# Down projections of four f blocks as seven products of halves in a hybrid decoder kernel

## The chip, the cores and the metric

The kernel runs on one core of a Trainium2 chip. The metric is the device time of one execution in microseconds (us); a profiled execution shows what each engine of the core did in it. The engines are TensorE (PE, with its weight loads as PEld), VectorE (DVE), ScalarE (ACT), GpSimd (POOL) and SyncE (SP), which here only issues DMAs.

## The reference, cut to what matters

Two decoder layers over 528 tokens (16 meta tokens and 512 others) with 1024 features. Each layer has an attention part, which the change leaves alone, and then a gated feed-forward part of 2816 hidden features, all in float32:

```python
h = h + mix @ w_out                                    # end of the attention part
hn = rmsnorm(h, ffn_norm)
ff = silu(hn @ w_gate) * (hn @ w_up)                   # 528 x 2816
h  = h + ff @ w_down                                   # 528 x 1024
```

After the second layer comes a last rmsnorm, and the meta tokens are dropped.

## The kernel before

Everything is kept transposed: features on the 128 partitions, tokens along the free axis. `h` is eight tiles of 128 x 528. The hidden features are 22 blocks of 128, called f; an output block of 128 features is called m. In the first layer a product covers 528 tokens, in two column halves of w = 264. In the second layer only the 512 real tokens count (w = 256).

A float32 product is made as three matmuls of rounded numbers. A weight tile or an activation is split into a high part (`hi`, a rounding copy on ACT) and a low part (`lo`, source minus high part, a subtraction on DVE or POOL), and hi x hi, hi x lo and lo x hi are added in PSUM. All "splits" below are such a pair: one ACT copy, then one DVE subtraction that waits for it.

The feed-forward part goes through `ROUNDS`: f blocks 0-2, 3-6, 7-10, 11-14, 15-18 and 19-21. The first three are computed plainly. Each later f is a `Unit`, which computes gate and up together: the 2 x 2 block product (two halves of the 1024 input features, two halves of the tokens, gate and up as the two outputs) is made by seven products instead of eight. The products are numbered 1, 2, 6, 5, 7, 4, 3 in the order in which they run; each is 12 matmuls. The banks are called x (products 1, 6, 7 and 4 add into it, and `keep` copies it out on ACT in between), z and y. `done` of a unit then adds the pieces, applies the scale `R` and silu, multiplies gate by up and splits the result into the activation tiles `ah` and `al` (f mod 8).

The down projection of a round is done while the next round's units run: a `down_job` loads the weights of two output blocks m for the round's f blocks, splits them, and `down` makes one m: for each f three passes over all tokens. In the first layer that is two 264-column matmuls per pass, in the second layer one of 512 columns. With four f blocks a pair of m takes 48 matmuls of 264 columns, or 24 of 512. Its result goes to an `S` tile (ACT) and is added to `h` by an accumulating DMA from GpSimd's queue. In the last round of units the addition is done by DVE, and the last round's own three f blocks are added after all units. The order before is: products 1, 2, 6, 5, 7 of the unit; first m; products 4 and 3 of the unit; second m.

The weights pass through jobs: `need(j)` loads and converts job j and the next two. A job's `hi` and `lo` live in two rings of two buffers each (`whi`, `wlo` and `fwhi`, `fwlo`, used in turn), so four jobs are alive at a time, and a fifth conversion waits until PE has finished the job four places before. The raw weights have a ring of three (`raw`), two (`fraw`) and two (`Sw`). For each unit two sums of weights are made by accumulating DMAs from GpSimd's queue (into `Sw` and `fraw`); DVE makes two more (`make2`, `make4`).

Tiles, slots and the order on each engine come from a scheduler that works on the program order and priorities; within an engine everything runs strictly in the order so fixed. PSUM has two double banks (`psd`) and four single banks (`psa`).

Of the kernel before, what the change touches and what calls it, by code (L numbers as in the profile page):

```python
# [10 lines left out]
F32 = mybir.dt.float32  # L11
# [28 lines left out]
def hybrid_kernel(ctx, tc, x_t, w_in, w_fl, w_out, w_gate, w_up, w_down, vecs, b_fg, rope, decay, mask, ident, out_t):  # L40
# [753 lines left out]
    def ffn(l, st, real, last):  # L794
# [6 lines left out]
        held = []  # L801
# [3 lines left out]

        def act_tile(f):
            return fft(f"ah{f % 8}"), fft(f"al{f % 8}")
# [80 lines left out]
        class Unit:  # L888
            def __init__(self, f):
                self.f = f  # L890
                self.t = {}
                self.w1 = add_job(load=self.load, make=self.make1, n=NK)

            def rest(self):
                self.w2 = add_job(load=self.load, make=self.make2, n=NK)
                self.w3 = add_job(load=self.load, make=self.make3, n=NK)

            def last(self):
                self.w4 = add_job(load=self.load, make=self.make4, n=HB)
# [15 lines left out]
            def make2(self, hi, lo):  # L915
                a, s = self.t["a"], self.t["s"]
                nc.vector.tensor_add(s[:, 0:HB], s[:, HB:NK], a[:, 0:HB])  # L917
# [8 lines left out]
            def make4(self, hi, lo):  # L926
                a, s = self.t["a"], self.t["s"]
                nc.vector.tensor_add(a[:, HB:NK], a[:, HB:NK], s[:, 0:HB])
                splits(hi, lo, a[:, HB:NK])
# [23 lines left out]
            def done(self):  # L953
# [12 lines left out]
                fh, fl = act_tile(self.f)  # L966
                split(fh[:, c], fl[:, c], u[:, c])
                acts[self.f] = (fh, fl)
# [12 lines left out]
            def tail(self):  # L981
                x, y = (self.bank(n) for n in "xy")
                return (product(self.w3, HB, t_form(3), x, False, True)
                        + product(self.w4, 0, x_block(1, 1), y, False, True, done=self.done))

# [51 lines left out]
        fills = []  # L1037
        for r, (f0, f1) in enumerate(ROUNDS):
            for f in range(f0, f1):
# [4 lines left out]
                u = Unit(f)  # L1044
# [16 lines left out]
            for p, g0, g1 in fills:  # L1061
                j = down_job(p, g0, g1)
# [353 lines left out]
```

## Time and profile before

| | before |
|---|---|
| median of 3 runs | 1272.64 us (1271.05 to 1273.75) |
| the profiled execution | 1271.96 us |
| its span | 1270.1 us |
| PE busy | 1255.0 us (99% of the span) |
| DVE busy | 914.1 us (72%) |
| ACT busy | 720.6 us (57%) |
| POOL busy | 386.2 us (30%) |
| first layer's feed-forward part | about 316 us, from 330 us to 646 us |
| second layer's | about 290 us, from 950 us to 1240 us |

The span is the time from the first to the last instruction in the profile; 1.9 us of the execution lie outside it. Busy time is the time in which an engine executes at least one instruction. Matmuls overlap in the array, so how long one takes in a row of them is read from the distance between their starts, and not from its own duration.

### The profile page before, as it was taken

The numbers are of one execution on the slowest core, as the hardware profiler recorded it, in microseconds if no ns is written. First come the engines' busy times: TensorE is split into PE (matmuls) and PEld (weight loads), VectorE is DVE, ScalarE is ACT, GpSimd is POOL, SyncE is SP. The second block draws the span as 40 slices with busy tenths as digits, with TensorE's granted clock in tenths as the row PEclk, the third lists the DMA queues.
The fourth block names the chain that finished last, engine by engine and source line by source line (L and its number), as shares of the span: only waits on it lengthen the run. The fifth ranks groups of instructions, "written<-read, shape, count | busy, mean of one in ns | idle before, by whom it ended". The sixth has DMA issues, their size and how long they took to land.

```text
span 1270.1 us, 24076 instructions
## 1 busy us (share of the span) xinstructions
PE 1255.0 (99%) x9271; PEld 1196.9 (94%) x9271; DVE 914.1 (72%) x1689; ACT 720.6 (57%) x1326; POOL 386.2 (30%) x662
## 2 busy tenths in 40 slices
PE   9999999999999999999999999999999999999997
PEld 8999999999999999999999989998789999999996
DVE  8877756779766666666786877477896666666766
ACT  7666545676555555554456665557765555555544
POOL 3355546421122222220025545554202222222100
PEclk9999999999999999999999999999999999999999
DMA  6322222225687777774323222222358887787721
GB/s 218 94 72 86 88 84 77 66 68 164 173 189 184 184 184 184 182 182 120 100 77 118 68 97 79 84 83 67 126 144 196 185 196 184 184 189 184 171 78 67
DMA packets 71315, 167.53 MB, mean 132 GB/s; under 512 B 8208, under 2 KB 15120, under 8 KB 71200
## 3 DMA queue, kind: packets, MB, share of 16 engines
q1 hardware_dynamic: 50576, 128.70, 31.7%
q0 software_dynamic: 20160, 36.97, 17.9%
q8 instruction: 73, 1.20, 0.4%
q14 instruction: 42, 0.34, 0.1%
q10 hardware_dynamic: 464, 0.32, 0.1%
HBM read 146.79 MB, written 2.13 MB: 117 GB/s over the span
## 4 chain that ended last, share of the span: by engine, by line
PE 92%; DVE 3%; DMA 2%; ACT 2%; issue 0%; DVEq 0%
PE psd L217 29%; PE psa L881 19%; PE psd L1016 14%; PE psd L881 13%; PE psa L217 5%; PE psa L1016 4%; PE psa L418 2%; PE psa L573 2%; PE psa L507 2%; PE psa L730 1%; PE psa L700 1%; DMA raw<-w_in 0%; DMA dec<-decay 0%; ACT whi L191 0%; PE psa L290 0%
## 5 line engine op out<-in xcount | busy, mean ns | idle before, releaser
L194 POOL TENSOR_TENSOR wlo<-raw,whi 128x128 fp32r<-128x128 f32 x504 | 259.1, 548 | 287.9 <-ACT whi L191 287.8
L217 PE MATMUL psd<-xh,whi 128*128 128x264 f32 (+1 forms) x792 | 195.8, 315 | 0.4 <-ACT whi L191 0.4
L217 PE MATMUL psd<-xh,wlo 128*128 128x264 f32 (+1 forms) x792 | 186.7, 303 | 0.0
L217 PE MATMUL psd<-xl,whi 128*128 128x264 f32 (+1 forms) x792 | 186.2, 302 | 0.4 <-DVE xl L320 0.4
L217 PEld LDWEIGHTS psd<-xh,whi 128*128 128x128 f32 x792 | 128.3, 189 | 5.4 <-ACT whi L191 1.1
L217 PEld LDWEIGHTS psd<-xh,wlo 128*128 128x128 f32 x792 | 127.0, 188 | 6.3 <-DVE wlo L194 0.4
L217 PEld LDWEIGHTS psd<-xl,whi 128*128 128x128 f32 x792 | 127.6, 189 | 4.7 <-DVE xl L320 0.8
L191 ACT CAST whi<-raw 128x512 fp32r<-128x512 f32 (+1 forms) x168 | 98.4, 613 | 49.6 <-PE psd L217 37.4
L908 POOL DMA_DIRECT2D Sw<-w_up x38 | 34.2, 899 | 230.5 <-DMA Sw<-w_up 146.4
L909 POOL DMA_DIRECT2D fraw<-w_gate x38 | 33.3, 875 | 210.5 <-DMA fraw<-w_up 65.9
L870 DVE TENSOR_TENSOR fwlo<-raw,fwhi 128x1024 fp32r<-128x1024 f32 (+2 forms) x62 | 64.0, 1033 | 38.1 <-ACT fwhi L869 38.0
L870 DVE TENSOR_TENSOR wlo<-raw,whi 128x1024 fp32r<-128x1024 f32 (+2 forms) x62 | 62.9, 1015 | 36.7 <-ACT whi L869 36.5
L869 ACT CAST whi<-raw 128x1024 fp32r<-128x1024 f32 (+2 forms) x62 | 54.9, 885 | 46.2 <-PE psd L881 37.0
L869 ACT CAST fwhi<-raw 128x1024 fp32r<-128x1024 f32 (+2 forms) x62 | 55.6, 897 | 42.8 <-PE psd L881 36.7
L917 DVE TENSOR_TENSOR Sw<-Sw,raw 128x512 f32<-128x512 f32 x38 | 26.3, 692 | 72.4 <-DMA raw<-w_gate 71.4
L1026 POOL DMA_DIRECT2D h<-S x64 | 59.9, 936 | 50.1 <-ACT S L1023 26.8
L881 PE MATMUL psa<-th,whi 128*128 128x264 f32 (+1 forms) x232 | 65.5, 283 | 0.0
L881 PE MATMUL psa<-th,wlo 128*128 128x264 f32 (+1 forms) x232 | 65.4, 282 | 0.0
L881 PE MATMUL psa<-tl,whi 128*128 128x264 f32 (+1 forms) x232 | 65.3, 282 | 0.0
L881 PE MATMUL psa<-th,fwhi 128*128 128x264 f32 (+1 forms) x224 | 63.5, 283 | 0.3 <-ACT e L947 0.3
L881 PE MATMUL psa<-tl,fwhi 128*128 128x264 f32 (+1 forms) x224 | 63.3, 283 | 0.0
L881 PE MATMUL psa<-th,fwlo 128*128 128x264 f32 (+1 forms) x224 | 63.2, 282 | 0.0
(344 smaller groups left out, 4027.3 us busy)
## 6 DMA issues: line engine op xcount, KB each, us to landing
raw<-w_in SPq DMA_DIRECT2D x54, 512.0 KB, 3.5
raw<-w_gate SPq DMA_DIRECT2D x44, 512.0 KB, 6.4
fraw<-w_up SPq DMA_DIRECT2D x38, 512.0 KB, 5.6
raw<-w_down SPq DMA_DIRECT2D x64, 256.0 KB, 2.9
Sw<-w_up SPq DMA_DIRECT2D x38, 256.0 KB, 2.6
fraw<-w_gate POOLq DMA_DIRECT2D x38, 256.0 KB, 4.3
Sw<-w_up POOLq DMA_DIRECT2D x38, 256.0 KB, 6.0
h<-S POOLq DMA_DIRECT2D x32, 264.0 KB, 5.5
```

Of the source, the lines that this page charges most:

```text
L191: pin(nc.scalar.copy(hi, job["raw"][:, c0:c1]), pinned)
L194: pin(sub(lo[:, i:i + step], job["raw"][:, c0 + i:c0 + i + step], hi[:, i:i + step].bitcast(F32)), pinned)
L217: nc.tensor.matmul(ps[1][b][:, 0:c1 - c0], w[:, wk, :], x[:, c0:c1], start=(k == 0 and i == 0), stop=(k == n - 1 and i == 2))
L418: nc.tensor.transpose(ps[:, 128 * j:128 * j + 128], src[:, o:o + 128], idt)
L869: nc.scalar.copy(hi, src)
L870: nc.vector.tensor_sub(lo, src, hi.bitcast(F32))
L881: nc.tensor.matmul(bank()[:, 0:b.shape[-1]], a[:, o + k, :], b, start=(fresh and k == 0 and i == 0), stop=(k == n - 1 and i == 2), skip_gr ...
L908: nc.gpsimd.dma_start(s[:, HB:NK], w_up[l, self.f][:, 0:HB], accum_op=ALU.add)
L909: nc.gpsimd.dma_start(self.t["b"][:, 0:HB], w_gate[l, self.f][:, 0:HB], accum_op=ALU.add)
L917: nc.vector.tensor_add(s[:, 0:HB], s[:, HB:NK], a[:, 0:HB])
L1016: nc.tensor.matmul(v[:, 0:c1 - c0], a[:, s * n + k, :], b[:, c0:c1], start=(k == 0 and i == 0), stop=(k == n - 1 and i == 2))
L1026: nc.gpsimd.dma_start(two(h[m]), c, accum_op=ALU.add)
```

## The change

Down projections of the four rounds with four f blocks (3-6, 7-10, 11-14, 15-18) are also made as a 2 x 2 block product by seven products. One `Down` covers two output blocks m (the two row halves), the even and the odd f blocks of the round (the inner halves; `w_down` is laid out in the order 0, 2, 1, 3 on the host for this) and the two halves of the tokens. Each product has two f blocks, so 6 matmuls; seven make 42. What this takes:

- Activations: for each pair of f blocks seven blocks of w columns are stored as hi and lo instead of four: the first unit's first half, both halves of the second unit, and four sums, which DVE makes (`done`: one subtraction after the first unit, three after the second). The splits cover 7 w per pair instead of 4 w.
- Weights: seven blocks of 128 x 256 instead of four. GpSimd makes three sums, as six additions of 128 x 128 (`Down.load`); DVE makes one, of 128 x 256 (`make_b`). The splits cover 1792 columns (two of 512, one of 768) instead of 1024. A `Down` is two jobs instead of one.
- Results: four ACT copies of w columns, one DVE addition of y to one of them (`keep`), and one DVE addition of z and y (`done`), before the accumulating DMAs to `h`, which stay two per pair. They are now also used in the last round of units, except for its last pair.
- Order: the products of the unit and of the `Down` alternate, as the tuples in the loop say; for the first pair of a round the last two products of the `Down` come after product 1 of the next unit. `need` looks three jobs ahead instead of two.
- A unit's `make4` addition is moved into `make2`; the raw gate weights have no later reader then.

```diff
         def need(j):
-            for i in range(j, min(j + 3, len(jobs))):
+            for i in range(j, min(j + (4 if jobs[j].get("far") else 3), len(jobs))):
...
                 nc.vector.scalar_tensor_tensor(lo, s, -1.0, hi.bitcast(F32), ALU.mult, ALU.subtract)
+                nc.vector.tensor_add(s[:, 0:HB], a[:, HB:NK], s[:, 0:HB])
...
             def make4(self, hi, lo):
-                nc.vector.tensor_add(a[:, HB:NK], a[:, HB:NK], s[:, 0:HB])
-                splits(hi, lo, a[:, HB:NK])
+                splits(hi, lo, self.t["s"][:, 0:HB])
...
+                q, second = divmod(self.f - PLAIN, 2)
+                if not second:
+                    us[q] = u2, two(tt("tq"))
+                    nc.vector.tensor_sub(us[q][1][:, 0], u2[:, 1], u2[:, 0])
+                    return
+                u0, ta = us.pop(q)
+                tb = two(tt("tq"))
+                parts = [(0, 1, u0[:, 0:1]), (1, 2, u2), (3, 2, ta), (5, 2, tb)]
+                for i, (s, n, src) in enumerate(parts):
+                    if i == 2:
+                        nc.vector.tensor_sub(tb[:, 0], u2[:, 1], ta[:, 0])
+                        nc.vector.tensor_sub(tb[:, 1], u2[:, 1], u0[:, 1])
+                        nc.vector.tensor_sub(ta[:, 1], u2[:, 0], tb[:, 0])
+                    ph, pl = slots(q, s, n, 0), slots(q, s, n, 1)
...
+        class Down:
...
+                for k in range(2):
+                    nc.gpsimd.tensor_add(sd[:, 2 + k], r[:, 4 + k], r[:, 6 + k])
+                for k in range(2):
+                    nc.gpsimd.tensor_sub(sd[:, k], sd[:, 2 + k], r[:, k])
+                for k in range(2):
+                    nc.gpsimd.tensor_sub(r[:, 4 + k], r[:, k], r[:, 4 + k])
+
+            def make_a(self, hi, lo):
+                splits(hi[:, 0:HB], lo[:, 0:HB], self.t["r"][:, 0:HB])
+                splits(hi[:, HB:NK], lo[:, HB:NK], self.t["s"])
+
+            def make_b(self, hi, lo):
+                r = self.t["r"]
+                nc.vector.tensor_sub(r[:, 2:4], r[:, 2:4], self.t["s"][:, 0:2])
+                splits(hi, lo, r[:, 2:NK])
...
+                        nc.scalar.copy(e, self.t["x"][:, 0:w])
+                        if i == 3:
+                            nc.vector.tensor_add(e, self.t["y"][:, 0:w], e)
...
+                    nc.vector.tensor_add(e, self.t["zy"][:, :, 0:w], e)
...
+                    if p == 0:
+                        order = ((u, 1), (u, 2), (u, 6), (u, 5), (u, 7), (d, 1), (d, 2), (u, 4), (d, 6), (d, 5), (u, 3), (d, 7))
+                    else:
+                        order = [(u, 1)] + hang + [(u, 2), (d, 1), (u, 6), (d, 2), (u, 5), (d, 6), (u, 7), (d, 5), (d, 7),
+                                                   (u, 4), (d, 4), (d, 3), (u, 3)]
+                    hang = [(d, 4), (d, 3)] if p == 0 else []
```

Three places show how the instructions now stand.

On DVE before, in the first layer, after a unit's up half is read from PSUM (L964, L965): w4's low part (L870 with 512 columns), the split of the activation (L143), then weights again.

```order
L964 TENSOR_TENSOR tq_5519<-psa_5365,tq_5519 128x264
L965 TENSOR_TENSOR tq_5519<-e_5378,tq_5519 128x264
L870 TENSOR_TENSOR fwlo_5620<-raw_5444,fwhi_5619 128x512
L143 TENSOR_TENSOR al7_5524<-tq_5519,ah7_5523 128x528
L870 TENSOR_TENSOR wlo_5647<-raw_5638,whi_5646 128x1024
L950 TENSOR_TENSOR e_5572<-psd_5574,e_5572 128x264
```

On DVE after, at the start of a round, behind the same two reads of PSUM (now L981, L982) of a round's last unit: `ab1` is a store of activation blocks, `raw_6203` and `nwt_6206` hold the weights of a `Down` and their sums, and `fwlo_6277` is the low part of its second job.

```order
L981 TENSOR_TENSOR tq_6187<-psa_6008,tq_6187 128x264
L982 TENSOR_TENSOR tq_6187<-e_6021,tq_6187 128x264
L1063 TENSOR_TENSOR raw_6203<-raw_6203,nwt_6206 128x256
L998 TENSOR_TENSOR tq_6191<-tq_6187,tq_6002 128x264
L999 TENSOR_TENSOR tq_6191<-tq_6187,tq_5998 128x264
L143 TENSOR_TENSOR ab1_4347<-tq_6187,ab1_4347 128x528
L1000 TENSOR_TENSOR tq_6002<-tq_6187,tq_6191 128x264
L887 TENSOR_TENSOR fwlo_6277<-raw_6203,fwhi_6276 128x768
L967 TENSOR_TENSOR e_6232<-psd_6234,e_6232 128x264
L143 TENSOR_TENSOR ab1_4347<-tq_6002,ab1_4347 128x528
L143 TENSOR_TENSOR ab1_4347<-tq_6191,ab1_4347 128x528
```

Where one split followed the reads, there are now three sums and three splits, with a sum and a split of down weights and an addition of a unit's y among them.

On GpSimd before, one unit and its pair of m in the first layer: DMAs only.

```order
L908 DMA Sw_5836<-w_up 128x512
L1026 DMA h1_74<-S_5552 128x528
L909 DMA fraw_5834<-w_gate 128x512
L1026 DMA h2_75<-S_5676 128x528
L908 DMA Sw_6030<-w_up 128x512
```

On GpSimd after, in a middle pair of a round, with the sums of down weights for the pair that follows (`nwt_5716`, `sqh_5927` and `raw` are the operands):

```order
L1051 TENSOR_TENSOR nwt_5716<-raw_5713 128x128 x2
L1053 TENSOR_TENSOR nwt_5716<-nwt_5716,raw_5713 128x128 x2
L1055 TENSOR_TENSOR raw_5713<-raw_5713 128x128 x2
L927 DMA fraw_5894<-w_gate 128x512
L1094 DMA h3_76<-S_5636 128x528
L926 DMA Sw_5896<-w_up 128x512
L1094 DMA h2_75<-S_5636 128x528
L1051 TENSOR_TENSOR sqh_5927<-raw_5924 128x128 x2
```

Six additions now stand in each unit between the DMAs, and the accumulation into `Sw` stands behind the first DMA to `h` of a pair, which waits for that pair's product 4.

On PE before, the first m of a pair stands behind product 7 of the unit (`psa_5947` is its x bank), at the start of a round:

```order
L881 MATMUL psa_5947<-th1_4307,fwhi_5943 128x264
L881 MATMUL psa_5947<-tl1_4308,fwhi_5943 128x264
L881 MATMUL psa_5947<-th1_4307,fwlo_5944 128x264
L1016 MATMUL psa_6038<-ah3_4789,whi_5978 128x264
L1016 MATMUL psa_6039<-ah3_4789,whi_5978 128x264
```

On PE after, at the same place: the unit's x bank is `psa_6219`, that of the `Down` is `psa_6307`, and its z and y are `psd_6316`. `ab0` holds the blocks of the round's first two f blocks and `ab1` those of the last two.

```order
L898 MATMUL psa_6219<-th1_4307,wlo_6168 128x264
L898 MATMUL psa_6307<-ab0_4346,fwhi_6213 128x264 x2
L898 MATMUL psa_6307<-ab0_4346,fwlo_6214 128x264
L898 MATMUL psa_6307<-ab1_4347,fwhi_6213 128x264 x2
L898 MATMUL psa_6307<-ab1_4347,fwlo_6214 128x264
L898 MATMUL psd_6316<-ab0_4346,fwhi_6213 128x264 x2
L898 MATMUL psd_6316<-ab0_4346,fwlo_6214 128x264
L898 MATMUL psd_6316<-ab1_4347,fwhi_6213 128x264 x2
```

A product of the `Down` reads blocks of the last two f blocks from its fourth matmul on, where before the last f block was read only after the three others.

More of the change, by code (lines that the diff above doesn't have):

```diff
@@ L1037, in ffn @@
         fills = []
+        hang = []
         for r, (f0, f1) in enumerate(ROUNDS):
@@ L1061, in ffn @@
             for p, g0, g1 in fills:
+                if r > 1:
+                    d = Down(p, r - 1, False)
+                    d.second()
+                    for i in (1, 2, 6, 5, 7, 4, 3):
+                        steps += d.p(i)
+                    continue
                 j = down_job(p, g0, g1)
@@ L1386 @@
     order = [0, 4, 1, 5, 2, 6, 3, 7]
+    forder = [f0 + i for f0, f1 in ROUNDS for i in ((0, 2, 1, 3) if f1 - f0 == 4 else range(f1 - f0))]
     wo = a["w_out"].reshape(DEPTH, 8, 128, D)[:, order].reshape(DEPTH, 2, 4, 128, 4, 2, 128).transpose(0, 1, 4, 3, 5, 2, 6).reshape(DEPTH, 2, 4, 128, 8, 128)
@@ L1394 @@
         "w_up": tiles(a["w_up"]),
-        "w_down": tiles(a["w_down"]),
+        "w_down": tiles(a["w_down"])[:, :, :, forder],
         "vecs": np.concatenate([col(a["attn_norm"]), col(a["ffn_norm"]), col(a["final_norm"]), col(a["ret_gn"])], 1),
```

119 lines of the change are left out of this document (107 added, 12 removed).

## Prediction

> **What bounds the kernel.** I read the busy times of the page first, then what PE waited for, then two stretches of one unit each (one per layer, in rounds with four f blocks).
>
> ```profile
> span 1270.1 us, 24076 instructions
> ...
> PE 1255.0 (99%) x9271; PEld 1196.9 (94%) x9271; DVE 914.1 (72%) x1689; ACT 720.6 (57%) x1326; POOL 386.2 (30%) x662
> ```
> ```profile
> PE psa L1268 <- DVE wide L61: 1.6, 1, 1.6
> ...
> PE psa L881 <- ACT e L947: 0.3, 1, 0.3
> ```
> ```profile
> 421.20:437.20 16.00, 16.00 (x134) 16.00 (x133) 10.42 (x15) 8.20 (x13) 3.48 (x4) 1.00 0.74 178
> 1041.50:1057.00 15.50, 15.50 (x109) 14.45 (x109) 10.40 (x15) 8.09 (x13) 3.45 (x4) 1.00 0.74 182
> ```
>
> The columns of the stretches are length, busy PE, PEld, DVE, ACT and POOL, granted clock, DMA share and GB/s. PE never rests in the units: of its listed waits only 0.3 us fall on their products (L881). DVE is busy 10.4 us of a unit's 16.0 us, or of 15.5 us in the second layer; POOL, with four DMA issues, 3.5 us. So matmuls taken away are worth their full time as long as DVE still keeps up.
>
> **What PE saves.** The pace is read from the chain that ended last and, for 256 columns, from two starts with 24 matmuls between them.
>
> ```profile
> 440.17 1.48 PE psa L881 x12
> 443.11 2.93 PE psd L1016 x24
> ...
> 1016.08 2.77 PE psd L1016 x12
> ```
> ```profile
> 1037.06 0.28 PE L881 MATMUL psa<-th,fwhi 128*128 128x256 f32 x1
> ...
> 1039.90 0.28 PE L881 MATMUL psa<-th,whi 128*128 128x256 f32 x1
> ```
>
> A matmul of 264 columns takes 2.93/24 = 0.122 us, one of 512 takes 2.77/12 = 0.231 us, one of 256 takes 2.84/24 = 0.118 us. In the first layer a pair of m goes from 48 to 42 matmuls: 6 x 0.122 = 0.73 us. In the second it goes from 24 x 0.231 = 5.54 us to 42 x 0.118 = 4.97 us: 0.57 us. With 16 pairs per layer that is 11.7 + 9.1 = **20.8 us**. A unit with its pair would take 15.3 us and 14.9 us.
>
> **What DVE gets.** Durations by form:
>
> ```profile
> L870 DVE TENSOR_TENSOR fwlo<-raw,fwhi 128x1024 fp32r<-128x1024 f32 x36 | 44.0, 1221 | 37.4 <-ACT fwhi L869 37.4
> ...
> L143 DVE TENSOR_TENSOR al<-tq,ah 128x528 fp32r<-128x528 f32 x22 | 15.6, 707 | 0.3
> ...
> L870 DVE TENSOR_TENSOR wlo<-raw,whi 128x512 fp32r<-128x512 f32 x20 | 13.8, 691 | 0.5 <-ACT whi L869 0.3
> ...
> L965 DVE TENSOR_TENSOR tq<-e,tq 128x264 f32<-128x264 f32 x19 | 8.1, 424 | 0.0
> ...
> L870 DVE TENSOR_TENSOR fwlo<-raw,fwhi 128x768 fp32r<-128x768 f32 x8 | 7.6, 955 | 0.6 <-ACT fwhi L869 0.6
> ```
>
> And one unit's end in order of time, with the last row of the chain in which product 3 gives way to the second m:
>
> ```profile
> 459.12 2.90 PE psd L1016 x24
> ```
> ```profile
> 459.85 0.70 DVE L957 TENSOR_TENSOR sg<-psd,e 128x528 f32<-128x528 f32 x1
> 460.47 1.22 DVE L870 TENSOR_TENSOR wlo<-raw,whi 128x1024 fp32r<-128x1024 f32 x1
> 461.60 0.70 DVE L959 SCALAR_TENSOR_TENSOR sg<-sg,R 128x528 f32<-128x528 f32 x1
> ...
> 464.04 0.70 DVE L962 SCALAR_TENSOR_TENSOR tq<-sg,R 128x528 f32<-128x528 f32 x1
> 464.78 0.43 DVE L964 TENSOR_TENSOR tq<-psa,tq 128x264 f32<-128x264 f32 x1
> 465.13 0.42 DVE L965 TENSOR_TENSOR tq<-e,tq 128x264 f32<-128x264 f32 x1
> 465.56 0.69 DVE L870 TENSOR_TENSOR fwlo<-raw,fwhi 128x512 fp32r<-128x512 f32 x1
> 466.25 0.71 DVE L143 TENSOR_TENSOR al<-tq,ah 128x528 fp32r<-128x528 f32 x1
> ```
>
> Back to back, starts lie about 0.08 us closer than the durations say (0.70 follows at 0.62, 1.22 at 1.13), so I count 1.14 us for 1024 columns, 0.87 for 768, 0.62 for 528, 0.61 for 512 and 0.35 for 264 or 256. Over two units (one pair of f blocks) DVE loses two low parts of 1024 (2.28) and two of 528 (1.24). It gains four low parts of 512 (2.44), two of 768 (1.74), two weight sums of 256 (0.70), two additions of y (0.70), two of z and y (1.24), four activation sums (1.40), and activation splits of one 264 and three 528 (2.21). That is 10.43 - 3.52 = 6.9 us for two units, so DVE stands at 10.4 + 3.5 = **13.9 us of 15.3 us** (first layer), and about 13.8 of 14.9. The moved `make4` addition costs the same in its new place. This is hidden behind PE only on the average, with 1.4 us to spare where 5.6 us were.
>
> ACT:
>
> ```profile
> L869 ACT CAST fwhi<-raw 128x1024 fp32r<-128x1024 f32 x36 | 37.8, 1049 | 24.6 <-PE psd L881 23.7 <-ACT e L947 0.6 <-DVE Sw L917 0.3
> ...
> L947 ACT COPY e<-psa 128x264 f32<-128x264 f32 x57 | 21.6, 379 | 14.3 <-PE psa L881 14.0
> ```
>
> It gets 768 more columns of weights and 396 of activations a unit, by the first row some 1.2 us, and up to 0.6 us for the smaller pieces and the four copies: 10.0 of 15.3 us, no bound. The accumulating DMAs to `h` stay two per pair; the bytes are the same, so a DMA share of 0.74 becomes 0.77.
>
> **GpSimd and its neighbour.** The price of the six additions is in the attention part, where POOL splits weights beside DVE:
>
> ```profile
> L194 POOL TENSOR_TENSOR wlo<-raw,whi 128x128 fp32r<-128x128 f32 x504 | 259.1, 548 | 287.9 <-ACT whi L191 287.8
> ```
> ```profile
> L194 POOL TENSOR_TENSOR wlo<-raw,whi x504: 445/461/2075, 21.9 to 896.4; 128x128 fp32r<-128x128 f32 x168
> ```
> ```profile
> L619 DVE TENSOR_TENSOR tq<-tq,xsw x16: 683/810/1016, 50.0 to 864.8; 128x528 f32<-128x528 f32 x12, 128x512 f32<-128x512 f32 x4
> ```
> ```profile
> L619 DVE TENSOR_TENSOR tq<-tq,xsw 128x528 f32<-128x528 f32 x12 | 9.8, 813 | 0.1
> ...
> L618 DVE TENSOR_TENSOR tq<-psd,cr 128x528 f32<-128x528 f32 x12 | 8.4, 700 | 0.0
> ```
>
> An addition of 128 x 128 on POOL takes 461 ns at the median and 548 ns on the mean, so POOL gets 3.3 us a unit and is at 6.8 of 15.3 us: no bound. But DVE pays: with both operands in SBUF (L619) 528 columns take 813 ns there against 707 ns in the feed-forward part (L143), while with one operand in PSUM (L618) they take 700 ns. The bounds for a unit are nothing (all six beside DVE's reads of PSUM or its pauses) and 6 x 0.461 = 2.8 us (each stops DVE for its own length). POOL computes in about half of the time there, so an operation that has it beside it throughout loses some 2 x 0.11 us; 3.3 us of POOL lie beside four of them: I take 0.9 us, since the row with the mean is the nearest. DVE then needs 14.8 of 15.3 us.
>
> The Trainium skill, "SBUF — State Buffer", section "SBUF: two separate sides", says that DVE with two SBUF inputs and a GpSimd operation hold the shared port pair one at a time and that the loser waits for the whole instruction. The rows agree on who is hit (L619, and not L618), and less on how much: the mean loss is 0.11 us, not 0.46. By the rule at its full length the sum would be that of the second rival below.
>
> **Where PE waits newly.** First, the start of a round. Before, the last f block's activation was read 18 + 84 matmuls after its unit ended (12 us). It was ready at 466.25 + 0.71 = 466.96, 7.8 us after product 3 ended at 459.12. Now the `Down` reads the second pair's block 1 at its product 2, 69 matmuls after the unit (8.4 us), and block 5 at product 6, 87 matmuls after it (10.6 us). DVE's row up to the split of block 1, in the order shown with the change and counted from L974: 0.62 + 1.14 + 0.62 + 1.22 + 0.62 + 0.61 + 0.70 + 0.35 + 0.70 + 0.62 = 7.2 us; it begins 0.7 us after the unit's end (459.85 against 459.12) and loses another 0.9 us to silu and ScalarE's high part, as before (7.1 us for 6.2 us of work). That is 8.8 us. Block 5 comes after 0.35 + 0.87 + 0.35 + 2 x 0.62 = 2.8 us more, at 11.6 us: 1.0 us late, 1.2 us with a part of POOL's additions. Rounds 11-14, 15-18 and 19-21 start so, in both layers (the round 7-10 has a further m of 18 matmuls ahead): 6 x 1.2 = **7 us**.
>
> Second, a steady unit. The sum into `Sw` now follows the first DMA to `h`:
>
> ```profile
> L917 DVE TENSOR_TENSOR Sw<-Sw,raw 128x512 f32<-128x512 f32 x38 | 26.3, 692 | 72.4 <-DMA raw<-w_gate 71.4 <-DMA Sw<-w_up 1.0
> ```
> ```profile
> DMA to landing us min/median/max: 4.2/6.0/10.8
> ```
> ```profile
> L1026 POOL DMA_DIRECT2D h<-S x64 | 59.9, 936 | 50.1 <-ACT S L1023 26.8 <-ACT S L1025 20.3 <-ACT e L947 2.0
> ```
>
> Product 4 of the `Down` ends 18 matmuls (2.2 us) before the unit; the copy takes 0.4 us, the issue to `h` 0.9 us, the sum lands 6.0 us after its own: 5.1 us after the unit's end. DVE comes to it after L979, 464.74 - 459.12 = 5.6 us after: hidden by half a microsecond at the median, 4 us late at the maximum. DVE waits there with the weights of the next unit behind it. With 0.5 us of play per unit I take 0.15 us for PE, between nothing and 0.5 us: 24 units, **3.5 us**.
>
> Third, each layer's end: the last pair runs alone, and its product 4 follows product 7 in the same bank, so PE waits for a copy (0.4 us and its signals); the last f block is then needed after 54 matmuls (6.6 us) instead of 84, against the 7.8 us above with less weight work in between: 1 us per layer, **2 us**.
>
> The sum is 20.8 - 7 - 3.5 - 2 = 8.3 us, from the profiled execution's 1271.96 us (its span and 1.9 us around it) to 1263.7 us. The median of the runs shown lies 0.7 us higher, so 1264 us.
>
> **Rivals.** (a) PE stays the only bound: the rings give enough lead, the round starts are covered, and all 20.8 us come: 1251 us. For it: PE's gapless row with a DVE at 65%. Against it: the 1.4 us to spare.
>
> (b) Slower: DVE becomes the bound because each of POOL's six additions stops it for 0.461 us. A unit then takes 13.9 + 2.8 = 16.7 us instead of 16.05, and 16.6 instead of 15.5: 12 x 0.65 + 12 x 1.1 = 21 us lost in the rounds that have both, some 2 us won in the last round of units: 1291 us, or 1283 with a third of the additions beside PSUM reads. It decides from about 2 us per unit on (16.05 - 13.9 and 15.5 - 13.8). For it: single operations of L619's kind take 1016 ns, 0.31 us more than alone; against it: their median of 810.
>
> (c) No change: the round starts cost 3 us each, because DVE carries a lag into them. Then 18 + 2 us eat the saving: 1271 us. For it: the chain from L974 is 11 us long in an order that cannot be altered; against it: the unit before a round's start has the smaller half of the activation work (one split of 264).
>
> That the change does nothing is excluded: the order shows the seven products of six matmuls.
>
> **Numbers.** My forecast (4 to 14 us won) 0.45, (a) 0.18, (b) 0.20, (c) 0.17, of which 0.12 within 0.2% (2.5 us, about what a measurement of this kernel can tell from no change), 0.02 faster and 0.03 slower. So faster 0.65, same 0.12, slower 0.23. The likeliest case alone spans 1258 to 1268 us. The range goes from (a), 1251 us, to 1282 us, inside (b), and leaves out the upper part of (b).
>
> **What would show it.** PE's idle time should be found at L898 with DVE's L143 (round starts) named as what it waited for, in stretches of about 1 us, six in all; a steady unit should take 15.3 to 15.6 us and 14.9 to 15.3 us, with DVE busy 14 to 15 us. If units take over 16 us with DVE at 99%, (b) holds; then L887's 512 columns should show well over 691 ns. If `Sw` is named by DVE's waits with more than 1 us a unit, the second term is too small. The forecast is wrong if PE waits for weights (L887) in steady units.

## The result and the profile after

The changed kernel takes 1305.73 us (median of 4 runs, 1304.82 to 1308.43), the kernel before 1272.22 us (median of 4 on the same chip): a ratio of 1.0266, 95% interval 1.0247 to 1.0285. The change makes the kernel 33 us slower. The prediction said 1264 us, and its range of 1251 to 1282 us does not reach this.

The head of the page after:

```profile
span 1303.0 us, 25214 instructions
...
PE 1253.1 (96%) x9463; PEld 1204.0 (92%) x9463; DVE 1029.1 (79%) x1942; ACT 774.6 (59%) x1502; POOL 540.9 (42%) x866
```

PE is busy about as long as before, in a span that is 33 us longer, and no other engine is near its limit on the average. So PE is kept waiting. First, where. The stretches below are bounded by the starts of ScalarE's copies of a unit's first x product (L947 before, L964 after). In each kernel the rows are the four units f 3 to 6 (round 1), the twelve units f 7 to 18 (the three rounds of four with a `Down` in every unit), and the same for the second layer. Columns: length, busy PE, PEld, DVE, ACT, POOL, granted clock, DMA share, GB/s. Before:

```profile
325.00:383.68 58.68, 58.68 (x485) 58.68 (x484) 39.81 (x55) 32.21 (x53) 13.03 (x15) 1.00 0.79 184
383.68:576.11 192.43, 192.43 (x1587) 192.43 (x1586) 125.69 (x169) 98.32 (x158) 42.28 (x49) 1.00 0.77 183
947.78:1005.54 57.76, 57.76 (x420) 54.51 (x418) 39.83 (x56) 31.61 (x48) 13.07 (x15) 1.00 0.80 191
1005.54:1191.10 185.56, 185.25 (x1290) 172.61 (x1290) 124.13 (x169) 96.63 (x145) 42.36 (x49) 1.00 0.80 188
```

After:

```profile
325.36:400.50 75.14, 63.97 (x492) 62.46 (x490) 42.36 (x63) 32.94 (x56) 16.91 (x21) 0.95 0.62 141
400.50:590.67 190.17, 187.66 (x1502) 186.10 (x1503) 168.10 (x266) 114.79 (x208) 97.78 (x121) 0.98 0.75 182
962.43:1036.71 74.28, 62.87 (x418) 58.20 (x417) 42.64 (x64) 32.20 (x52) 16.91 (x21) 0.94 0.63 146
1036.71:1222.15 185.44, 180.41 (x1506) 178.50 (x1505) 167.92 (x266) 113.63 (x208) 97.59 (x121) 1.00 0.76 185
```

Round 1 went from 58.7 to 75.1 us and from 57.8 to 74.3 us: 33.0 us, the whole loss. These units run no seven-product `Down` at all. The twelve units that do are 2.3 us faster in the first layer and 0.1 us in the second, where 8.8 (12 x 0.73) and 6.8 us (12 x 0.57) were expected. The rest of the span is 2.3 us longer. So there are two questions: what broke round 1, and where the later rounds' gain went.

What PE and DVE waited for, after (total us, times, longest):

```profile
PE psd L898 <- DVE sg L974: 18.4, 7, 4.1
PE psd L898 <- DVE S L1085: 7.0, 10, 1.4
PE psa L898 <- ACT e L964: 4.8, 7, 0.9
PE psa L898 <- ACT S L1083: 4.5, 6, 1.4
PE psa L898 <- DVE ab L143: 0.5, 1, 0.5
```
```profile
DVE Sw L935 <- DMA Sw<-w_up: 31.2, 6, 8.1
DVE Sw L935 <- issue: 27.1, 4, 8.6
```

PE waits for a unit's gating (L974, which empties its PSUM tile), and DVE stands 58.3 us, in ten places, at the sum L935 of `make2`, waiting for `Sw`; eight of the ten, with 54.0 us, lie in round 1. Before, it waited 1.0 us in all for that tile's transfer and 71.4 us for the gate weights, in pauses of up to 3.3 us. One of the ten in order of time, DVE after:

```profile
337.90 1.22 DVE L937 SCALAR_TENSOR_TENSOR wlo<-Sw,whi 128x1024 fp32r<-128x1024 f32 x1
...
344.31 0.69 DVE L887 TENSOR_TENSOR fwlo<-Sw,fwhi 128x512 fp32r<-128x512 f32 x1
...
347.83 0.42 DVE L967 TENSOR_TENSOR e<-psd,e 128x264 f32<-128x264 f32 x1
356.88 0.69 DVE L935 TENSOR_TENSOR Sw<-Sw,raw 128x512 f32<-128x512 f32 x1 [8.62 <-issue]
357.49 1.22 DVE L937 SCALAR_TENSOR_TENSOR fwlo<-Sw,fwhi 128x1024 fp32r<-128x1024 f32 x1
358.62 0.70 DVE L974 TENSOR_TENSOR sg<-psd,e 128x528 f32<-128x528 f32 x1
```

SP's and POOL's queues in the same stretch, after:

```profile
345.02 0.33 SPq L925 DMA_DIRECT2D Sw<-w_up  x1
```
```profile
350.53 0.87 POOL L927 DMA_DIRECT2D fraw<-w_gate  x1 [7.25 <-DMA fraw<-w_up]
352.12 0.87 POOL L926 DMA_DIRECT2D Sw<-w_up  x1 [0.73 <-DMA Sw<-w_up]
```

The row at 337.90 is `make2`'s remainder of a unit; the one at 344.31 is the same unit's w4, now read from the same `Sw`. SP starts the load of the unit after the next into this buffer at 345.02, the moment w4's low part (344.31 + 0.69) has read it. The load, GpSimd's accumulation behind it and its landing take until 356.88; DVE has come to the sum at 348.25 (347.83 + 0.42) and stands for 8.6 us. Behind it in its row stand the remainder of the unit that runs and its gating (L974), for which PE waits. The same place before, DVE and SP:

```profile
346.44 0.68 DVE L928 TENSOR_TENSOR raw<-raw,Sw 128x512 f32<-128x512 f32 x1
...
350.09 1.23 DVE L919 SCALAR_TENSOR_TENSOR fwlo<-Sw,fwhi 128x1024 fp32r<-128x1024 f32 x1 [0.83 <-ACT fwhi L918]
...
363.82 0.69 DVE L917 TENSOR_TENSOR Sw<-Sw,raw 128x512 f32<-128x512 f32 x1 [2.11 <-DMA raw<-w_gate]
```
```profile
351.35 0.33 SPq L907 DMA_DIRECT2D Sw<-w_up  x1
```

There w4's addition (L928) reads `Sw` too, but it stands ahead of the remainder and writes `raw`. So the load starts when `make2`'s remainder (L919) has read `Sw`, 12.5 us ahead of the sum, and DVE does not wait for this transfer. The change writes w4's addition into `Sw`, so the tile stays taken until w4's split: to 345.00 instead of 339.12 (337.90 + 1.22). Of two buffers one is held 5.9 us longer, the sum's lead shrinks to 3.2 us (348.25 - 345.02), and the transfer takes 11.9 us. Each unit ends later for it, so the next starts as late.

### The profile page after: what moved, and what is told of

It reads as the page before. It is cut to its first block, busy times and chain, and to the rows that moved or that the text cites. A ratio compares the mean times of both kernels' runs of the same rounds, so it can differ in the third digit from the quotient of the medians.

```text
span 1303.0 us, 25214 instructions
## 1 busy us (share of the span) xinstructions
PE 1253.1 (96%) x9463; PEld 1204.0 (92%) x9463; DVE 1029.1 (79%) x1942; ACT 774.6 (59%) x1502; POOL 540.9 (42%) x866
## 4 chain that ended last, share of the span: by engine, by line
PE 70%; DVE 13%; DMA 7%; issue 6%; ACT 3%; POOL 1%; DVEq 0%; POOLq 0%; ACTq 0%; SPq 0%
PE psd L217 28%; PE psa L898 17%; PE psd L898 12%; PE psa L217 4%; DMA Sw<-w_up 4%; PE psa L418 2%; DMA fraw<-w_up 2%; DVE fwlo L887 2%; PE psa L573 2%; PE psa L507 2%; DVE wlo L887 1%; PE psa L730 1%; PE psa L700 1%; DVE wlo L937 1%; DVE sg L974 1%
## 5 line engine op out<-in xcount | busy, mean ns | idle before, releaser
L217 PE MATMUL psd<-xh,whi 128*128 128x264 f32 (+1 forms) x792 | 196.0, 315 | 0.5 <-ACT whi L191 0.5
L887 DVE TENSOR_TENSOR wlo<-raw,whi 128x1024 fp32r<-128x1024 f32 (+2 forms) x66 | 75.8, 1148 | 16.3 <-ACT whi L886 16.1
L898 PE MATMUL psa<-th,fwhi 128*128 128x264 f32 (+1 forms) x256 | 74.4, 291 | 1.5 <-ACT e L964 1.5
L898 PE MATMUL psa<-tl,fwhi 128*128 128x264 f32 (+1 forms) x256 | 73.8, 288 | 0.0
L898 PE MATMUL psa<-th,fwlo 128*128 128x264 f32 (+1 forms) x256 | 73.7, 288 | 0.0
L935 DVE TENSOR_TENSOR Sw<-Sw,raw 128x512 f32<-128x512 f32 x38 | 27.1, 712 | 58.4 <-DMA Sw<-w_up 31.2
L964 ACT COPY e<-psa 128x264 f32<-128x264 f32 (+1 forms) x114 | 42.7, 375 | 44.5 <-PE psa L898 44.5
L898 PE MATMUL psd<-xh,whi 128*128 128x264 f32 (+1 forms) x186 | 54.1, 291 | 13.6 <-DVE sg L974 13.6
L142 ACT CAST ab<-tq 128x528 fp32r<-128x528 f32 (+1 forms) x64 | 36.1, 573 | 51.5 <-DVE tq L982 27.3
L527 ACT ACTIVATE probs<-probs,nmax 128x144 f32<-128x144 f32 (+1 forms) x64 | 36.9, 576 | 44.3 <-DVE nmax L514 31.5
L887 DVE TENSOR_TENSOR fwlo<-raw,fwhi 128x512 fp32r<-128x512 f32 (+2 forms) x52 | 45.9, 883 | 20.1 <-ACT fwhi L886 20.0
L898 PE MATMUL psa<-th,whi 128*128 128x264 f32 (+1 forms) x200 | 57.3, 287 | 3.4 <-ACT e L964 3.4
```

The lines of the kernel that those rows point to most:

```text
L142: pin(nc.scalar.copy(hi, src), pinned)
L217: nc.tensor.matmul(ps[1][b][:, 0:c1 - c0], w[:, wk, :], x[:, c0:c1], start=(k == 0 and i == 0), stop=(k == n - 1 and i == 2))
L527: nc.scalar.activation(pr, pr, AF.Exp, bias=nmax[0:nq], scale=-1.0, accum_out=rsum)
L887: nc.vector.tensor_sub(lo, src, hi.bitcast(F32))
L898: nc.tensor.matmul(bank()[:, 0:b.shape[-1]], a[:, o + k, :], b, start=(fresh and k == 0 and i == 0), stop=(k == n - 1 and i == 2), skip_gr ...
L964: nc.scalar.copy(self.t["e"][:, i], self.t["x"][:, 0:w])
```

## The experiments

Theory T1: the addition into `Sw` holds the ring. Rival R1: round 1 suffers from what else is new there, the sums of the activation pairs on VectorE and their buffers. The "before" of each ratio is the kernel before, run beside (1272.1 to 1273.4 us). "The kernel of 1275.6 us" in the expectations is the one with the early addition into raw.

### What broke round 1

**The addition alone, in the kernel before.** Edit:

```
 def make2:  ... lo from s, hi
+    nc.vector.tensor_add(s[:, 0:HB], a[:, HB:NK], s[:, 0:HB])
 def make4:
-    nc.vector.tensor_add(a[:, HB:NK], a[:, HB:NK], s[:, 0:HB]); splits(hi, lo, a[:, HB:NK])
+    splits(hi, lo, s[:, 0:HB])
```


> The kernel before with one edit of the change alone: the w4 addition is made in make2 and written into the sum's tile Sw, and make4 splits from there. Down projections and activations stay as before. Theory T1 (the addition holds Sw until w4's split, so the next load into that ring starts late, and VectorE, in order, stands at the next unit's sum ahead of this unit's own gating): round 1 of each layer loses about 16 us as in the changed kernel, and the later rounds, where this kernel's order also puts the next sum ahead of this unit's w3 work, lose too: 1305 us at least, up to 1390. Theory R1 (round 1 is slow because VectorE now makes the pair sums of the activations there, or because of the activations' new buffers): none of that is here, so 1272 us plus or minus 4.

1405.05 us, ratio 1.1041 (1.1024 to 1.1057): T1, somewhat above its upper end, because most units stall. Its waits of DVE and of PE:

```profile
DVE Sw L917 <- issue: 205.4, 28, 9.1
```
```profile
PE psd L881 <- DVE sg L956: 52.6, 28, 4.0
```

One moved addition, which neither adds nor removes work, costs 133 us.

**The old addition back, in round 1 and in all rounds.** `if self.far` (true from round 2 on) selects the new form in the first kernel; the second has the old form everywhere.

> The changed kernel, with the old place and the old buffer of the w4 addition (made at w4, into raw) for the units of round 1 only; all later rounds as changed. T1: round 1 of each layer goes back from 75 us to about 59 us for its four units, so 1306 minus 33 is 1273 us (1268 to 1278), and VectorE's waits for Sw by the sum nearly vanish in round 1. R1 (pair sums on VectorE, new buffers): those stay, so 1303 to 1306 us.

> The changed kernel with the old place and buffer of the w4 addition in all units. T1: round 1 is mended (minus 33 us), but in rounds 2 to 5 the ring raw, which the down weights share, is held until w4 again, so the down weights come later than they do now; each of the 16 pairs then loses something between 0 and 7 us: 1273 to 1385 us, and whatever is above 1273 is what the early addition buys in the later rounds. R1: round 1 stays at 75 us, so at least 1305 us.

1279.82 us (1.0054, 1.0039 to 1.0069) and 1281.12 us (1.0071, 1.0045 to 1.0097). Round 1 is back at 59.9 to 61.1 us. 26 of the 33 us are won; the total stays above T1's 1268 to 1278 because single units elsewhere lost some. The two kernels differ by 1.3 us, less than their own runs do: the early addition buys nothing measurable in the later rounds, where it was the reason for the move (`raw` free sooner for the down weights).

**Early, but into the other buffer; and a third `Sw`.** In the first kernel round 1 alone writes `raw`, the later rounds still write `Sw`, and `make4` splits from `d4`. In the second a scratch tile of the activations' forms gets four rows instead of six, to make room. Edits:

```
 (first)  + d4 = self.t["d4"] = s[:, 0:HB] if self.far else a[:, HB:NK]
          + nc.vector.tensor_add(d4, a[:, HB:NK], s[:, 0:HB])
 (second) - fft("Sw", F32, (128, NK, 128), 2)
          + fft("Sw", F32, (128, NK, 128), 3)
```


> The changed kernel; in round 1 alone the w4 addition stays early, in make2, but is written into raw (as before) and not into Sw. This tells the time of the addition apart from the buffer that it holds. T1 says the buffer: Sw is free after the negated copy and its remainder again, round 1 is mended, 1273 us (1268 to 1278), as with the late addition. If it is the place of the addition in VectorE's row (0.7 us ahead of work that is waited for): 1300 us or more. R1: 1303 to 1306 us.

> The changed kernel exactly in its arithmetic and its order, with a third buffer for Sw (room for it: the scratch S of the activations' forms has four rows instead of six, two of its rows stand in the tile e). T1 (the addition in make2 holds the Sw ring, two buffers, until w4's split): the load of the next Sw no longer waits for that split, so the 33 us of the two first rounds come back, 1270 to 1278 us. If something else than the ring makes round 1 slow, 1300 us or more.

1275.58 us (1.0045, 1.0022 to 1.0067) and 1280.18 us (1.0068, 1.0053 to 1.0083). It is the buffer, not the time of the addition. The second time is 2 us above T1's range, but with three buffers round 1 is as before within 1 us, although the pair sums, the splits and the early addition into `Sw` are all there:

```profile
324.18:382.78 58.60, 58.60 (x484) 58.60 (x483) 42.12 (x63) 32.96 (x56) 16.36 (x21) 1.00 0.77 176
945.12:1003.78 58.66, 56.99 (x413) 53.68 (x412) 41.99 (x64) 32.41 (x52) 15.79 (x21) 1.00 0.78 180
```

R1 falls for this kernel. Its later rounds lost 1.9 us (round 4 of the first layer) and 2.9 us (round 2 of the second) against the kernel with the addition into `raw`; why was not taken apart.

### Where the later rounds' gain went

The mended kernel (early addition into `raw`) is the base: 3 us slower than before, where the forecast was 8 us faster.

**T2, the order at the second pair.** In its first layer each round's second pair took 16.8 to 18.1 us (16.8 are its products' time), with PE waiting up to 1.1 us for the addition of the kept y. Edit: the first pair's last two products one place later.

```
-order = [(u, 1)] + hang + [(u, 2), (d, 1), (u, 6), (d, 2), ...
+order = [(u, 1), (u, 2)] + hang + [(u, 6), (d, 1), (d, 2), ...
```


> The kernel with the early addition into raw in round 1 (1275.6 us), and one change of order more: the last two products of the first pair's Down run after the next unit's product 2, not before it. Theory T2: the loss at each round's second pair is TensorE waiting (0.6 to 1.05 us a round, with little cover: one product of 1.5 us) for VectorE's addition of the kept y, which stands in VectorE's row behind the remainder of the sum (1.21 us) and behind a remainder that waited 1.0 us for ScalarE. With product 2 (2.9 us) as cover the waits for the S tile go: 6 rounds times about 0.8 us, so 1270 us (1267 to 1273). Rival R2 (the sums of the down weights on GpSimd come late by themselves, whatever stands around): the wait comes back at a later product, 1274 to 1278 us.

1278.62 us (1.0055, 1.0038 to 1.0072). T2's 1270 is wrong. PE's waits, in the base and then in this kernel:

```profile
PE psd L898 <- DVE S L1086: 5.2, 7, 1.1
PE psa L898 <- ACT S L1084: 4.5, 7, 1.4
```
```profile
PE psa L898 <- ACT S L1084: 6.3, 5, 2.5
PE psd L898 <- DVE S L1102: 3.7, 6, 0.8
...
PE psd L898 <- DVE S L1086: 1.1, 3, 0.5
```

The wait that the edit covered went from 5.2 to 1.1 us, and others took its place. PE's wait is only where a late DVE shows.

**No sums; sums on DVE; no pair sums.** Edits: `load` without GpSimd's six operations and the splits from `r` directly; the same three sums in `make_a` on `nc.vector`; the four subtractions of each activation pair dropped, with the tiles that they write.

> As the kernel of 1275.6 us, with the six GpSimd sums of every pair's down weights left out (the halves are split as they were loaded; VectorE's and ScalarE's work is the same). R2 and the rival of the prediction with GpSimd's additions slowing VectorE at 0.9 us a unit: without them at least 8 us are won, 1267 us or less. T2: only the 1.0 us that ScalarE and VectorE wait for the sums at each second pair goes, 1269 to 1273 us. If neither the sums nor their contention cost anything: 1275 us.

> As the kernel of 1275.6 us, with the sums of the down weights on VectorE, in three operations of 128x512, 128x512 and 128x512 elements (0.6 us each by the rows of the trace, so 1.9 us for each pair), none on GpSimd. If GpSimd's additions cost VectorE about as much as they save (0.9 us a unit), this is within 3 us of 1275.6 us; T2, which finds VectorE's row short of time at the second pair, says 1.9 us more there for each of 12 pairs that are not first: 1280 to 1295 us.

> As the kernel of 1275.6 us, with the sums of each pair's activations left out (four operations on VectorE, 1.6 to 1.8 us per pair of units; the splits stay and take other rows). If what round 1 still lost against the kernel before (1.1 us in layer 1, 2.6 us in layer 2) and the later units' 0.3 us come from VectorE's load: 1268 to 1272 us. If VectorE has room and only the order in its row counts: 1273 to 1276 us.

1260.26 us (0.9905, 0.9892 to 0.9917), 1274.33 us (1.0018, 1.0008 to 1.0028) and 1263.91 us (0.9928, 0.9915 to 0.9940). GpSimd's six additions per pair cost 15.3 us of time. On DVE the sums cost 14.1, for 28.4 us of busy time (1035.2 against 1006.8 without sums); a part of this may be DVE's waits for the down weights there, 16.2 us in all. My expectation had priced them at twice their size, for they are 128x256 each (419 ns by their rows, 0.3 us of busy time). The activations' subtractions, 27.5 us of DVE's busy time (1030.3 to 1002.8), cost 11.7 us, more than either reading had said. So DVE's work counts about half of its length, although DVE is busy only 81% of the span.

**More lead for the down weights.** A fourth `raw` buffer, with the sums on GpSimd and on DVE.

> The kernel with the early addition into raw in round 1 (1275.6 us), with four buffers for raw instead of three (same room). Leaving the sums of the down weights out won 15 us, and GpSimd stands 61 us before its first sum waiting for the down weights to land. Theory T2a (lateness: the down weights are loaded only when raw is free, so sums, high parts and remainders are late at the second pair): with a fourth buffer they land earlier and about 6 us at the second pairs of layer 1 and 2 come back, 1264 to 1270 us. Theory T2b (GpSimd's additions slow VectorE, 23.5 us of busy time less over 32 pairs without them, whenever they run): 1273 to 1277 us.

> Four buffers for raw, and the sums of the down weights on VectorE in three operations of 128x256 per pair (0.3 us each by busy time, 28.4 us in all, where GpSimd's cost VectorE 23.5 us). T2a: the lateness goes and nothing is left of GpSimd's slow additions in the chain, 1262 to 1268 us. T2b: VectorE has about the same load as before, so 1272 to 1276 us.

1341.87 us (1.0537, 1.0508 to 1.0565) and 1329.37 us (1.0457, 1.0432 to 1.0481): both theories missed. DVE waits, in the first:

```profile
DVE Sw L935 <- DMA Sw<-w_up: 89.3, 22, 6.8
```

With a further buffer the order of transfers on SP's and GpSimd's queues is another one, and DVE waits for `Sw` in 22 units. So this says nothing on lateness of the down weights; it says again that `Sw` is the tightest transfer.

**Latency or contention.** Three kernels take the sums' cost apart: sums made into a tile that nobody reads; one addition of 128x1 in their place, which waits for the same landing; and, for latency, the splits of the summed half issued later.

> As the kernel of 1275.6 us, but GpSimd's six additions per pair are made into a tile that nothing reads; the halves are split as they were loaded (so as in the kernel without sums, 1260.3 us, plus GpSimd's additions at the place and time that they have). It tells the two ways in which the sums cost 15 us apart. Latency (ScalarE and VectorE wait for the sums, and what stands behind them in VectorE's row is late): the time falls to 1260 to 1264 us. Contention (the additions make VectorE's operations longer, 23.5 us of busy time): it stays at 1271 to 1276 us.

> As the kernel whose sums are made but not read (1277.1 us), with one GpSimd addition of 128x1 elements per pair in place of the six of 128x128. It reads both halves of the down weights, so GpSimd waits for their landing as long as before, and the DMA starts behind it in GpSimd's row (h, Sw, fraw) come as late; only the time in which its additions read and write beside VectorE is gone. Contention: 1259 to 1264 us, as without sums. GpSimd's row (the wait for the landing holds up its DMA starts): 1272 to 1278 us.

> As the kernel of 1275.6 us, with the splits of the summed half of the down weights issued after the first product of the Down instead of with the first half's, so that a late sum holds up less behind it in the rows of ScalarE and VectorE. Latency: 1265 to 1272 us where the rows move, 1275 us where the scheduler puts the splits at the same places. Contention: 1274 to 1277 us.

Unused sums: 1277.06 us (1.0035, 1.0019 to 1.0050). One column instead of 128: 1261.46 us (0.9917, 0.9904 to 0.9931). Later splits: 1277.66 us (1.0039, 1.0022 to 1.0056). So nobody waits for a sum to any effect, and GpSimd's own wait for the weights does no harm: it is still 118 us in the kernel with one column. What costs is that the additions run. What they do to DVE stands in the rows by form. Base:

```profile
L887 DVE TENSOR_TENSOR wlo<-raw,whi 128x1024 fp32r<-128x1024 f32 x34 | 45.4, 1334 | 15.6 <-ACT whi L886 15.6
...
L143 DVE TENSOR_TENSOR ab<-tq,ab 128x512 fp32r<-128x512 f32 x24 | 18.1, 756 | 1.0 <-ACT ab L142 1.0
...
L887 DVE TENSOR_TENSOR fwlo<-Sw,fwhi 128x512 fp32r<-128x512 f32 x22 | 17.3, 788 | 4.9 <-ACT fwhi L886 4.9
...
L975 DVE TENSOR_TENSOR sg<-psd,e 128x512 f32<-128x512 f32 x19 | 12.9, 681 | 0.0
```

With one column:

```profile
L887 DVE TENSOR_TENSOR wlo<-raw,whi 128x1024 fp32r<-128x1024 f32 x34 | 41.6, 1223 | 20.6 <-ACT whi L886 20.4
...
L143 DVE TENSOR_TENSOR ab<-tq,ab 128x512 fp32r<-128x512 f32 x24 | 16.3, 683 | 1.0 <-ACT ab L142 1.0
L887 DVE TENSOR_TENSOR fwlo<-Sw,fwhi 128x512 fp32r<-128x512 f32 x22 | 15.1, 688 | 5.6 <-ACT fwhi L886 5.4
...
L975 DVE TENSOR_TENSOR sg<-psd,e 128x512 f32<-128x512 f32 x19 | 13.0, 682 | 0.0
```

In these forms operations with both inputs in SBUF take 73 to 111 ns more on the mean in the base, those with one in PSUM (L975) nothing. Forms that seldom meet an addition take nothing more either (`fwlo<-fraw` of 128x1024: 1216 and 1217 ns). Single rows of the base show more than the means, first two of DVE, then what GpSimd does beside them:

```profile
564.07 1.23 DVE L887 TENSOR_TENSOR wlo<-raw,whi 128x1024 fp32r<-128x1024 f32 x1 [0.66 <-ACT whi L886]
...
992.50 2.60 DVE L983 TENSOR_TENSOR tq<-e,tq 128x256 f32<-128x256 f32 x1
```
```profile
564.13 1.91 POOL L1052 TENSOR_TENSOR nwt<-raw 128x128 f32<-128x128 f32 x2 [6.24 <-DMA raw<-w_down]
...
993.67 1.14 POOL L1056 TENSOR_TENSOR raw<-raw 128x128 f32<-128x128 f32 x2
```

In the first place GpSimd loses: the first of the two additions takes 1.48 us, where the eighteen that have no operation of DVE beside them take 0.46 us at the median; it ends 0.31 us after DVE's. In the second DVE loses: an operation of 0.41 us takes 2.60 us and ends after the last of the six additions (994.81).

DVE's busy time falls from 1030.3 to 1006.5 us: 23.8 us over 32 pairs, 0.74 us per unit. One thing this pair of kernels does not tell apart: without the additions GpSimd's own row is also 3.8 us a pair shorter, and DVE's waits for `Sw` fall from 7.3 to 1.1 us, so a part of the 15 us may be DMAs that start late behind the additions. In the first layer the twelve units of the base stand against those with one column, which are what the matmuls alone give:

```profile
384.11:572.58 188.47, 186.30 (x1512) 184.38 (x1511) 169.00 (x266) 115.32 (x209) 94.73 (x121) 1.00 0.76 183
```
```profile
386.26:570.34 184.08, 184.08 (x1512) 183.98 (x1511) 160.71 (x266) 115.29 (x208) 48.24 (x61) 1.00 0.77 188
```

184.08/12 = 15.34 us a unit, PE without a pause; in the second layer it is 178.09/12 = 14.84 us.

**Tries for a faster kernel.** Three `Sw` with the later splits; GpSimd's sums as three of 128x256; three `Sw` with the sums on DVE; and the sums on DVE with the first of the three made by an accumulating DMA (`sd[:, 2:4]` loaded with two blocks of the odd weights, the other two added by the transfer).

> The same on the kernel with three Sw buffers (1280.2 us), whose first rounds take 58.6 us in both layers as in the kernel before. Latency: 1266 to 1274 us. Contention: 1278 to 1282 us.

> As the kernel of 1275.6 us, with GpSimd's six sums of 128x128 made as three of 128x256. By its own rows (128x128 takes 0.46 us alone, 128x544 1.37 us) a sum of 256 would take about 0.74 us for 0.92, so the sums are ready 0.5 us earlier per pair and GpSimd holds the memory about 0.5 us less: latency 1272 to 1275 us, contention 1271 to 1274 us, so this tells little apart and is run for the time.

> The changed kernel with three Sw buffers (1280.2 us, its first rounds 58.6 us in both layers) and with the sums of the down weights on VectorE (three operations of 128x256 per pair), which in the other kernel gave 1274.3 us with 59.9 and 61.4 us in the first rounds. Were the two gains to add up: 1268 to 1272 us, faster than the kernel before. If VectorE's load in the later rounds eats it: 1273 to 1280 us.

> As the kernel with the sums on VectorE (1274.3 us), with the first of the three made by the transfer itself: two blocks of the odd down weights are loaded into the sum's tile and the other two are added by an accumulating transfer, 256 KB more per pair, and VectorE makes two sums of 128x256 instead of three. VectorE has 0.3 us less for each of 32 pairs, 9.5 us in all; at the share that VectorE's 28.4 us cost (14 us of time), 4 to 5 us come back: 1268 to 1271 us, faster than the kernel before. If the transfers, 0.61 to 0.84 of their engines' time in these rounds, come late with 256 KB more per unit: 1276 to 1300 us.

1278.50 us (1.0048, 1.0036 to 1.0061), 1283.38 us (1.0076, 1.0061 to 1.0090), 1288.64 us (1.0126, 1.0108 to 1.0144) and 1270.61 us (0.9992, 0.9979 to 1.0005). The first three are slower than the kernel before by 0.5 to 1.3%. The merged sums and the sums on DVE with three `Sw` came out above both values that their expectations named, and the gains of three `Sw` and of sums on DVE do not add up. The last has the lowest median of those that leave nothing out, and cannot be told from the kernel before. None beats it. That taking work off DVE and GpSimd is the way, and that 1260 us is there when the sums cost nothing, is shown by the kernels that leave them out, not by a whole one.

## Why the prediction was wrong

- **The step that failed** is one sentence: "The moved `make4` addition costs the same in its new place." Its 0.6 us do. But its new output is `Sw`, and I did not ask what that write holds up: a DMA two queues away (SP's load, then GpSimd's accumulation), and with it DVE's row in the next unit. It cost 26 to 30 us, by the kernels in which round 1 writes `raw` again (1279.82 and 1275.58 us against 1305.73). No rival had it.
- **The `Sw` term** ("hidden by half a microsecond at the median", 3.5 us over 24 units) looked at the right transfer in the wrong round. I costed units with a pair, where the sum stands behind L979 in the order after; in round 1 it stands ahead of the unit's gating, and I neither read that order nor costed units without a `Down`, since nothing seemed to change there. In the units that I costed the term was not too small: there DVE waited for `Sw` at two sums, 1.95 and 2.27 us. The other 54.0 of the 58.3 us lie in round 1.
- **PE's saving was right.** Forecast 0.73 us a pair in the first layer and 0.57 in the second: without the additions the twelve units take 184.08 instead of 192.43 us, 0.70 us each, and 178.09 instead of 185.56 us, 0.62 each.
- **The contention's size was right, its effect was not.** Forecast 0.9 us of DVE per unit from L619's mean, measured 0.74. I took it as hidden by DVE's free time but for 0.2 us at six round starts. The additions cost 15 us, two thirds of DVE's 23.8 us, with what GpSimd's longer row may add. A mean load of 14.8 in 15.3 us is no cover; the likely reason, which no run isolates, is that DVE's row moves in bursts behind waits for high parts and transfers, and PE's tiles have little slack. Rival (b) had this mechanism with 21 us, by a unit's mean exceeding PE's; that is not how it came, since DVE is busy only 14.1 us of a unit's 15.7 (169.00 us over twelve units of 188.47 in the base). Its 1283 us for a third of the additions beside PSUM reads does not follow from its own terms either: 13.9 + 1.9 = 15.8 us is still under the 16.05 us from which it counts a loss.
- **The round starts** lost about what was said, at another place: not at the start behind the activations' splits (L143: 0.5 us in all) but in the second pair's unit, up to 1.4 us each, behind the additions into `S` (L1085: 7.0 us, where 7 us were forecast). That the sums agree is luck: it is another wait. Without GpSimd's additions they take their products' 16.8 us.
- The Trainium skill's rule of the shared port pair ("SBUF — State Buffer", section "SBUF: two separate sides") is borne out in who is hit: L975, with one input in PSUM, is not. Its wait for the whole instruction is not seen in the means, 73 to 111 ns per operation of DVE, but it is in the single rows: 1.48 us for an addition of 0.46 us, 2.60 us for an operation of 0.41 us. The means are smaller because GpSimd is often the one that waits, and because many operations of DVE meet no addition or only the end of one: L887 of 128x1024 takes 1.38 us where an addition runs beside it, 1.22 us elsewhere.

## What to carry to other kernels

Where an edit changes the tile that an instruction writes, ask first whose buffer it is and which transfer waits for that buffer: the cost lies there and not in the instruction. Look at the units that the change does not mean to touch as closely as at those it does. An engine at 90% of a unit's time is already part of the bound where its row is in order and PE's PSUM tiles wait for it: price added work there at about half of its length (0.43 to 0.64 in these kernels), and take no average load for cover.

## What the hardware showed unexpectedly

After a pause of some 3 us PE ran slowly for a while: a row of the changed kernel's chain right after the last pause of round 1 against one in steady work, and the stretch of the first with its granted clock of 0.50.

```profile
400.93 3.01 PE psa L898 x12
...
419.16 2.21 PE psa L898 x18
```
```profile
400.90:406.60 5.70, 5.67 (x25) 5.67 (x26) 5.70 (x10) 2.34 (x5) 5.08 (x8) 0.50 0.89 221
```

3.01/12 = 0.251 us a matmul and 2.21/18 = 0.123: half speed. The trace's clock records show it five times in the two first rounds, behind pauses of 2.89, 2.98, 3.05, 3.50 and 4.09 us (from the modelled end of one matmul to the start of the next), each time for 3.41 or 6.83 us. In the first layer's round 1 this is up to a third of the loss: PE is busy 63.97 us for the same products that took 58.68, beside 11.2 us of pauses. So each of these pauses costs PE more than its own length. The Trainium skill ("TensorE: Matmul & The Clock Gate", section "Part 1: The HAM clock gate (the "warmup" mystery)") gives the gate two states, full and half speed, the latter after an idle window of about 3.4 us. The 0.251 us agree with the half; here a pause of 2.89 us was enough.

GpSimd pays for the contention as well. Two rows by form of its additions in the base:

```profile
L1056 POOL TENSOR_TENSOR raw<-raw 128x128 f32<-128x128 f32 x64 | 47.6, 767 | 0.0
L1052 POOL TENSOR_TENSOR sqh<-raw 128x128 f32<-128x128 f32 x32 | 27.3, 870 | 65.8 <-DMA raw<-w_down 65.6
```

Over all five such rows, 192 additions, the mean is 767 ns, from 655 to 870. The additions with no operation of DVE beside them take 457 ns at the median: one loses some 0.3 us on the mean, more than an operation of DVE.
